# Hybrid pooling and short-convolution block, 256 tokens by 4096 channels: the parked gate product, the corner sums and the turned quarter share one 8 KB tile, and small work is moved in time

## The chip, the core and the metric
The kernel runs on one core of one Trainium2 chip. Time is device time in microseconds (us). The kernel before takes 2443.77 us, the median of three runs (2441.69 to 2444.59).

Engines: TensorE (PE; PEld is its load of the stationary operand), VectorE (DVE), ScalarE (ACT), GpSimd (POOL) and SyncE (SP). SP and POOL here mostly issue DMAs, each in the order of its own queue. Each engine executes its instructions in program order, so an instruction that waits holds up all behind it on that engine.

## The reference, cut to what matters
```python
def reference(x, norm_w, w_in, pool_w, pool_scale, conv_w, conv_b, gate_b, w_branch, w_out, final_norm_w):
    b, s, d = x.shape                                   # 1, 256, 4096
    for l in range(DEPTH):                              # 1
        h = rmsnorm(x, norm_w[l])
        proj = jnp.einsum('bsd,de->bse', h, w_in[l])    # 4096 -> 20480
        u_p, z_p, u_c, b_c, c_c, z_c, g_logit = jnp.split(proj, SPLIT_POINTS, axis=-1)
        y_pool = causal_multiscale_pool(u_p, pool_w[l], pool_scale[l]) * jax.nn.silu(z_p)
        y_conv = causal_gated_shortconv(u_c, b_c, c_c, conv_w[l], conv_b[l]) * jax.nn.silu(z_c)
        ys = jnp.stack([y_pool, y_conv], axis=2)
        br = jnp.einsum('bsnc,ncd->bsnd', ys, w_branch[l])          # 2 x (2048 -> 4096)
        gates = jax.nn.sigmoid(g_logit.reshape(b, s, N_BRANCHES, d) + gate_b[l])
        merged = jnp.sum(gates * br, axis=2)
        x = x + jnp.einsum('bsd,de->bse', merged, w_out[l])
    return rmsnorm(x, final_norm_w)
```
All is float32. The two branches (`n` = 0 pooling, 1 convolution) are each multiplied by a gate and added: `merged = g0*p0 + g1*p1`, 4096 channels wide.

## The kernel before, in words
**Units and steps.** Every matrix product is cut into units of 1024 output columns, and a unit into steps of 256 input channels. The units, in order: the convolution branch's `cz0 cb0 cu0 cc0 cz1 cb1 cu1 cc1`, the pooling branch's `pz0 pu0 pz1 pu1`, the gates `g0_0 g1_0 g0_1 ... g1_3` (branch, column quarter), the branch products `b0_0 b1_0 b0_1 ... b1_3`, and the output `o0` to `o3`. Units of w_in and w_out have 16 steps, branch units 8. A plain step (P) has 24 matmuls of 128x512, each float32 product being three products of rounded high and low halves; a step of Strassen's kind (S) has 21, seven products in place of eight. A text such as `SIX4` or `B0` gives a unit's steps; the gates' usual unit has 360 matmuls, `g1_3`, `cz1`, `pz0` and `o0` have 366, a `b0` unit ("PPPPPSPS") 186 and a `b1` unit ("PSPSPSPP") 183.

**Weights.** SP loads each step's 1 MB of weights into `raw`, three slots used in rotation. For a step, ACT rounds the weights to the high halves (`highs`, L54, `ring<-raw`) and DVE subtracts to get the low halves (`lows`, L57, `ring<-raw,ring`) into `ring`, 15 cells, of which a P step takes 4 and an S step 3 + 4. For S steps DVE first makes four sums in `parts`. A slot of `raw` is free for the next load when the step's lows are made; a cell of `ring` when the matmuls have read it. Preparation runs at most some three steps ahead of PE.

**The ends of units.** Banks `sums` (E) and `shared` (F) collect the results. At a unit's end ACT copies the E banks to `E` (or `Y`): `E<-sums`. The F banks ("corners") are copied to a slot, summed there by DVE (`corner_sums`) and added to `E` (`combine`). That slot (`join`) is one of the three of `raw`, in its turn in the rotation, unless `rotates` is off: the `b0` units use the tile `last_pair` (8 KB a partition).

**Work beside the product.** A unit's epilogue is a list of items; one is issued every tick (TICK, six matmuls). `silu`, transposes, the three taps of the convolution (`taps(j)`, four pairs of channel blocks, in `cz1` for `cc0` and in `pz0` for `cc1`), the bias gathers and sigmoids of the gates are such items. Gates are stored to `gates_d` in DRAM and come back later. In a `b0` unit's epilogue the product E*Y (branch times gate) is parked in `last_pair`; in a `b1` unit's it is E*Y, plus the parked product, then transposed on PE and stored to `m_d`. Both gates are loaded into Y (`before`), after the seventh of eight steps of the unit they belong to.

**Operands.** The stationary operands lie in `arena` (one more in `last_pair`, region LAST): first x, replaced by y (both branches' results, from `y_d`) during `g1_3` and `b0_0`, and by the merged rows (from `m_d`) from `b0_3` to `o0`. A `Fill` fetches 256 KB by POOL into `sa` or `sb`; at the earliest LANDING ticks later it is worked off one phase a tick: for a plain operand ACT rounds, then DVE subtracts; for one of S kind DVE makes four sums, ACT rounds, DVE subtracts.

**Opening.** In `cz0` x comes in 16 pieces in the order FIRST; pieces 0 to 7 are plain (`x_direct`), 8 to 15 staged (`x_scale` on ACT, `x_sums` on DVE, before the step that uses them). The rows of x, four of 1 MB, are fetched into E for the sum of squares (`fetch_rows`, `square`).

Of the kernel before, what the change touches and what calls it, by code (L numbers as in the profile page):

```python
# [10 lines left out]
F32R = mybir.dt.float32r  # L11
BF16 = mybir.dt.bfloat16
AF = mybir.ActivationFunctionType
# [6 lines left out]
NU = 1024  # L20
# [11 lines left out]
TAIL = 3  # L32

SIX5 = "PPPPPSPSPSPSPSPS"
FIRST = (0, 8, 9, 1, 10, 11, 2, 12, 13, 3, 14, 15, 4, 5, 6, 7)
OPENED = 10
SIX4 = "PPPPSPSPSPSPSPSP"
SEVEN3 = "PPPSPSPSPSPSPSPS"
EIGHT = "PSPSPSPSPSPSPSPS"
# [7 lines left out]
def hybrid_block(ctx: ExitStack, tc: tile.TileContext, x, xc, prm, rows_in, w_in, pool_w, w_branch, w_out, out):  # L47
# [5 lines left out]
    def act(dst, src, func=AF.Copy, **kw):  # L53
        return pin(nc.scalar.activation(dst, src, func, **kw))  # L54
# [4 lines left out]
    def mul(dst, a, b):  # L59
        return tt(dst, a, b, ALU.mult)  # L60

    def add(dst, a, b):
        return tt(dst, a, b, ALU.add)

    def sub(dst, a, b):
        return tt(dst, a, b, ALU.subtract)
# [7 lines left out]
    def move(dst, src):  # L74
        return pin(nc.gpsimd.dma_start(dst, src))
# [15 lines left out]
    E = sb("E", [P, 2, NU])  # L91
    Y = sb("Y", [P, 2, NU])
# [11 lines left out]
    gates_d = dram.tile([2, 4, P, 2, NU], F32, name="gates_d")  # L104
    g_d = dram.tile([2, P, 2, NU], F32, name="g_d")
    y_d = dram.tile([2, 2, P, 4, 2, T], F32, name="y_d")
    m_d = dram.tile([4, P, 4, 2, T], F32, name="m_d")
    o_d = dram.tile([3, P, 2, NU], F32, name="o_d")

    xrows = xf.rearrange("(t p) d -> p t d", p=P)  # L110
# [254 lines left out]
    def shared(i):  # L365
        return PF[i]
# [48 lines left out]
    def transposes(src, done):  # L415
        items = []
        for j in range(4):
            def f(j=j):
                for i in range(2):
                    for t in range(2):  # L420
                        c = (2 * j + i) * P
                        pin(nc.tensor.transpose(shared(j)[:, i * T + t * P:i * T + (t + 1) * P],  # L422
                                                src[:, t, c:c + P], ident))
                done(j)
            items.append(f)
        return items

    def pairs(items):
        return [lambda a=a, b=b: (a(), b()) for a, b in zip(items[::2], items[1::2])]

    def put(dst, src):
        for k in range(2):
            move(dst[:, :, 1 - k], src.rearrange("p (q k) t -> p q k t", k=2)[:, :, k])

    def chan(tile_):
# [12 lines left out]
    def make_ops(kinds):  # L448
# [33 lines left out]
    def conv_units(c, first):  # L482
        base = 2 * HALF + c * NU

        def b_epi(u):
            def copy(j):
                act(chan(Y)[:, 2 * j:2 * j + 2], bankview(j))
            return gap(6) + transposes(E, copy) + [lambda: move(g_d[c], Y)]

        def c_epi(u):  # L490
            def copy(j):
                if j == 3:
                    for i in range(4):
                        act(chan(E)[:, 2 * i:2 * i + 2], bankview(i))

            def taps(j):
                v, y = chan(E)[:, 2 * j:2 * j + 2], chan(Y)
                for i in range(2):
                    b = 2 * j + i
                    kb = 8 * c + b  # L500
                    act(y[:, b], v[:, i], AF.Identity, scale=tap_col(2, kb), bias=bias_col(kb))
                for i in range(2):
                    b = 2 * j + i
                    kb = 8 * c + b
                    for s in (1, 2):
                        stt(y[:, b, s:], v[:, i, 0:T - s], tap_col(2 - s, kb), y[:, b, s:], ALU.mult, ALU.add)

            items = gap(6) + pairs(transposes(E, copy)) + gap(2)
            for j in range(4):
                items += [lambda j=j: taps(j), None]  # L510
            return items + [lambda: move(E, g_d[c])] + gap(6) + [lambda: mul(Y, Y, E), lambda: put(y_d[1, c], chan(Y))]

        in_unit(f"cz{c}", base + 3 * HALF, lambda u: silu_y(), FIRST if first else SIX4, dst=Y)
        in_unit(f"cb{c}", base + HALF, b_epi, EIGHT).urgent = lambda: mul(E, E, Y)
        in_unit(f"cu{c}", base, lambda u: gap(2) + band_items(0) if c == 0 else [], SEVEN3, dst=Y)
        in_unit(f"cc{c}", base + 2 * HALF, c_epi, EIGHT).urgent = lambda: mul(E, E, Y)
# [100 lines left out]
    def gate_unit(n, c):  # L617
        def epi(u):
            def bias(t):
                gather(E[:, t], gate_b[n, None, c * NU:(c + 1) * NU].to_broadcast([P, NU]))  # L620

            return gap(1) + [lambda: bias(0), lambda: bias(1)] + gap(12) + [
                lambda: act(E[:, 0], E[:, 0], AF.Sigmoid), None,
                lambda: act(E[:, 1], E[:, 1], AF.Sigmoid), lambda: move(gates_d[n, c], E)]
        text = HOST if (n, c) == (0, 0) else SIX4 if (n, c) == (1, 3) else EIGHT
        in_unit(f"g{n}_{c}", 6 * HALF + n * D + c * NU, epi, text)

    def branch_unit(n, c):
        def epi(u):
            if n == 0:  # L630
                return gap(1) + [lambda: mul(parked_sum(), E, Y)]

            def copy(j):
                act(chan(Y)[:, 2 * j:2 * j + 2], bankview(j))

            def stored():
                put(m_d[c], chan(Y))
                merged[c] = now[0] + STORED
            return [lambda: mul(E, E, Y), None, add_parked] + gap(11) + pairs(transposes(E, copy)) + [stored]

        def add_parked():
            add(E, E, parked_sum())
            if c == 3:
                last_pair["stack"].close()
                open_last(F32R)
                last_pair["dtype"] = F32R

        text = B1 if n else B0
        u = Unit(f"b{n}_{c}", lambda i: w_branch[n, c, i], seq_y(text), y_ops[n], epi,
                 before=lambda: move(Y, gates_d[n, c]))  # L650
        u.urgent, u.lead = (lambda: None), 3
        if n == 0:
            u.rotates = False
        units.append(u)

    def parked_sum():
        return last_pair["tile"].rearrange("p (a n) -> p a n", a=2)

    merged = {}

# [25 lines left out]
    def copy(dst, src):  # L686
        return pin(nc.vector.tensor_copy(dst, src))
# [7 lines left out]
    class Fill:  # L695
# [9 lines left out]
        def advance(self):  # L705
            o, q = self.o, self.st[:, 0:self.o.n] if self.o.kind == "S" else self.st[:, 4:8]
            if self.phase == 0 and o.kind == "S":
                sums_s(self.st)
                self.phase = 1
            elif self.phase < 2:  # L710
                act(o.view[:, 0], q)
                self.phase = 2
            else:
                sub(o.view[:, 1], q, o.view[:, 0].bitcast(F32))
                self.phase = 3
                o.ready = True
                fills.remove(self)
# [1 line left out]
    stages = [sa]  # L719
    fills = deque()  # L720
    now = [0]
    LANDING, STORED = 6, 7

    def pop_fill(force=None):
        now[0] += 1
# [43 lines left out]

    def freed(o):  # L770
        if o.region == LAST:
            return lambda: "dtype" in last_pair
        return lambda: all(p.left == 0 for p in o.prev)

    warm = op.tile([P, 2 * P], BF16, name="warm")
# [17 lines left out]
        stt(r, m, 1.5, r, ALU.add, ALU.mult)  # L793

    def fetch_rows(c):
        move(E, xrows[:, :, c * NU:(c + 1) * NU])

    def square(c):
        q = E
# [2 lines left out]

    first_order = FIRST
    xt = Y.rearrange("p a n -> p (a n)").rearrange("p (s o c) -> p s o c", s=4, c=P)
# [194 lines left out]
    for u in units:  # L999
# [129 lines left out]
```

## Time and profile before
| | |
|---|---|
| median of 3 runs | 2443.77 us |
| the profiled execution's own time | 2441.96 us |
| its span, first to last instruction | 2440.2 us |
| mean granted clock of TensorE | 0.993 |
| PE busy, 10515 matmuls | 2382.4 us, 98% |
| DVE busy | 2130.3 us, 87% |
| ACT busy | 1430.8 us, 59% |
| POOL busy | 86.3 us, 4% |
| DMA moved | 547.07 MB, 224 GB/s mean |

The sum of the prediction is made against the profiled execution (2441.96 us, of which 1.8 us lie around the span). In the views, "a<-b" is what an instruction writes and reads, by the program's names; the helpers ACT L54 and DVE L57 record nearly everything those engines do, so groups are told apart by tiles. Idle time stands in brackets with what ended it. The view of stretches of time gives, for each engine, busy time and number of instructions in that stretch, then the granted clock, the DMA engines' busy share and GB/s.

### The profile page before, as it was taken

The page shows a single profiled execution, that of the slowest core. Times are in us where ns is not written, and L with a number is a line of the kernel's source. Part 1 is how long each engine was busy: PE and PEld are TensorE (multiplying, and loading weights), DVE is VectorE, ACT ScalarE, POOL GpSimd, SP SyncE. Part 2 cuts the span into 40 slices and gives each one's busy share as a digit, 9 for nine tenths or more (in the row PEclk, how much of TensorE's full clock was granted, in tenths as well). Part 3 has the DMA queues.
Part 4 walks back from the last instruction along what each step waited for, and adds up shares of the span by engine and source line. Part 5 has one row for each costly group of instructions (what it writes and reads, how often), then busy time and mean ns, then how long its engine had stood idle before and what let it go on. Part 6 is the DMA issues. An engine that isn't in the chain of part 4 may idle for free. (4 is left out here: it accounts for less than half of the span.)

```text
span 2440.2 us, 26870 instructions
## 1 busy us (share of the span) xinstructions
PE 2382.4 (98%) x10515; PEld 1959.1 (80%) x10515; DVE 2130.3 (87%) x1756; ACT 1430.8 (59%) x1380; POOL 86.3 (4%) x148
## 2 busy tenths in 40 slices
PE   8999999999999999999999999999899999899998
PEld 6888887888878888888888888887678887778886
DVE  8789989988989879879999999888788789799998
ACT  5655656656556556556666566655555556456664
POOL 0000000000000000000000000000000001000000
PEclk9999999999999999999999999999999999999999
DMA  8656556555646555555676567667656656658667
GB/s 320 232 190 228 194 187 245 215 205 192 226 182 229 207 206 191 207 208 193 238 258 236 197 239 256 225 211 256 221 214 251 250 204 235 216 197 281 236 222 265
DMA packets 82959, 547.07 MB, mean 224 GB/s; under 512 B 9488, under 2 KB 9488, under 8 KB 21776
## 3 DMA queue, kind: packets, MB, share of 16 engines
q1 hardware_dynamic: 69120, 484.47, 54.2%
q0 software_dynamic: 13280, 59.78, 7.9%
q8 instruction: 82, 1.34, 0.2%
q10 hardware_dynamic: 432, 1.11, 0.1%
q14 instruction: 45, 0.37, 0.0%
HBM read 519.10 MB, written 26.21 MB: 223 GB/s over the span
## 5 line engine op out<-in xcount | busy, mean ns | idle before, releaser
L935 PE MATMUL sums<-ring,arena 128*128 128x512 f32 x7515 | 1760.0, 391 | 38.2 <-ACT E L54 17.9
L935 PEld LDWEIGHTS sums<-ring,arena 128*128 128x128 f32 x7515 | 1411.4, 188 | 340.7 <-DVE ring L57 21.9
L57 DVE TENSOR_TENSOR ring<-raw,ring 128x2048 fp32r<-128x2048 f32 (+3 forms) x526 | 938.8, 1796 | 186.4 <-ACT ring L54 182.7
L54 ACT ACTIVATE ring<-raw 128x2048 fp32r<-128x2048 f32 (+3 forms) x526 | 790.7, 1519 | 491.5 <-PE sums L935 259.5
L54 ACT ACTIVATE ring<-parts 128x1024 fp32r<-128x1024 f32 (+1 forms) x403 | 399.9, 1007 | 355.4 <-DVE parts L57 322.8
L935 PE MATMUL shared<-ring,arena 128*128 128x512 f32 x2100 | 509.5, 391 | 5.0 <-DVE ring L57 5.0
L57 DVE TENSOR_TENSOR ring<-parts,ring 128x2048 fp32r<-128x2048 f32 (+3 forms) x225 | 434.9, 1945 | 50.3 <-ACT ring L54 49.4
L935 PEld LDWEIGHTS shared<-ring,arena 128*128 128x128 f32 x2100 | 395.4, 189 | 91.0 <-DVE ring L57 8.7
L57 DVE TENSOR_TENSOR parts<-parts,raw 128x512 f32<-128x512 f32 x378 | 262.0, 693 | 12.9
L57 DVE TENSOR_TENSOR parts<-raw 128x1024 f32<-128x1024 f32 x189 | 230.6, 1220 | 8.0 <-DMA raw<-in_w_in_dram 7.1
L935 PE MATMUL sums<-ring,last_pair 128*128 128x512 f32 x366 | 89.8, 396 | 0.0
L935 PEld LDWEIGHTS sums<-ring,last_pair 128*128 128x128 f32 x366 | 68.9, 188 | 16.5
L57 DVE TENSOR_TENSOR raw<-raw 128x512 f32<-128x512 f32 (+1 forms) x78 | 67.7, 868 | 11.1 <-ACT raw L54 9.3
L54 ACT ACTIVATE raw<-shared 128x512 f32<-128x512 f32 x104 | 55.8, 606 | 2.8 <-DVE ring L57 2.1
L54 ACT ACTIVATE E<-sums,rin 128x512 f32<-128x512 f32 x56 | 36.4, 686 | 25.5 <-PE sums L935 25.4
L935 PE MATMUL shared<-ring,last_pair 128*128 128x512 f32 x168 | 41.6, 396 | 0.0
L935 PEld LDWEIGHTS shared<-ring,last_pair 128*128 128x128 f32 x168 | 31.6, 188 | 7.7
L69 DVE SCALAR_TENSOR_TENSOR E<-raw,rin,E 128x1024 f32<-128x1024 f32 x28 | 34.7, 1280 | 0.2
L54 ACT ACTIVATE arena<-sa 128x512 fp32r<-128x512 f32 (+2 forms) x16 | 12.2, 760 | 32.9 <-DMA sa<-y_d 15.1
L78 POOL DMA_DIRECT2D E<-in_rows_dram x16 | 13.9, 867 | 432.9 <-DVE E L69 430.8
L54 ACT ACTIVATE arena<-sb 128x512 fp32r<-128x512 f32 (+1 forms) x15 | 11.3, 754 | 25.8 <-DVE sb L57 20.9
L57 DVE TENSOR_TENSOR E<-E,Y 128x2048 f32<-128x2048 f32 x11 | 25.2, 2290 | 0.3
(116 smaller groups left out, 566.8 us busy)
## 6 DMA issues: line engine op xcount, KB each, us to landing
raw<-in_w_in_dram SPq DMA_DIRECT2D x319, 1024.0 KB, 4.8
raw<-in_w_branch_dram SPq DMA_DIRECT2D x64, 1024.0 KB, 4.9
raw<-in_w_out_dram SPq DMA_DIRECT2D x64, 1024.0 KB, 5.0
E<-in_rows_dram POOLq DMA_DIRECT2D x16, 512.0 KB, 11.3
gates_d<-E POOLq DMA_DIRECT2D x8, 1024.0 KB, 8.3
Y<-gates_d POOLq DMA_DIRECT2D x8, 1024.0 KB, 6.2
Y<-in_xc_dram SPq DMA_DIRECT2D x16, 256.0 KB, 5.9
E<-in_x_dram POOLq DMA_DIRECT2D x4, 1024.0 KB, 6.5
```

The lines of the kernel that those rows point to most:

```text
L54: return pin(nc.scalar.activation(dst, src, func, **kw))
L57: return pin(nc.vector.tensor_tensor(out=dst, in0=a, in1=b, op=op))
L69: return pin(nc.vector.scalar_tensor_tensor(out=dst, in0=a, scalar=s, in1=b, op0=op0, op1=op1, **kw))
L78: return pin(nc.gpsimd.dma_start(dst, src, accum_op=ALU.add))
L935: pin(nc.tensor.matmul(ps, lhs, rhs, start=n == 0, stop=n == u.total[b] - 1))
```

## The change
Seven edits, in the order of the words in the diff:

1. FIRST takes the pieces of x in another order: the second step's piece is now a plain one, and staged pieces stand at places 2, 4, 6, 7, 9, 10, 12, 14 (counted from 0) in place of 1, 2, 4, 5, 7, 8, 10, 11. OPENED goes from 10 to 12 with it.
2. The four `taps` stand at ticks 11, 17, 25 and 33 of the epilogue in place of 11, 13, 15 and 17.
3. `p0`, the first branch times its gate, stays in Y (`Y = E*Y`). `last_pair` takes in turn: the corners of both branches, the second gate, and the turned quarter (for c < 3; the last one is turned in Y). So `b1` units too have `rotates` off, and no slot of `raw` serves as corner slot from `b1_0` to `b1_3`.
4. The gates' loads move: the first gate of quarter 0 is loaded right after the last gate is stored, those of quarters 1 to 3 at the twelfth tick of the `b0` unit before use; the second gate is loaded into `last_pair` at the first tick after the `b1` unit. Its product (`gated`) is at tick 8 and the sum with Y at tick 9, where both were in ticks 1 and 3. The transposes stay where they were.
5. A fill of S kind is rounded by DVE (`copy`, a cast) in the same tick as its subtraction; ACT no longer takes part.
6. LANDING goes from 6 to 8 ticks.
7. The first row fetch of x goes through SP (`load`), where it stands behind the loads of the first seven weight tiles; the other three stay on POOL.

```diff
-FIRST = (0, 8, 9, 1, 10, 11, 2, 12, 13, 3, 14, 15, 4, 5, 6, 7)
-OPENED = 10
+FIRST = (0, 1, 8, 2, 9, 3, 10, 11, 4, 12, 13, 5, 14, 6, 15, 7)
+OPENED = 12
...
-            items = gap(6) + pairs(transposes(E, copy)) + gap(2)
-            for j in range(4):
-                items += [lambda j=j: taps(j), None]
+            items = gap(6) + pairs(transposes(E, copy)) + gap(1)
+            for j, n in enumerate((1, 5, 7, 7)):
+                items += gap(n) + [lambda j=j: taps(j)]
...
-                lambda: act(E[:, 1], E[:, 1], AF.Sigmoid), lambda: move(gates_d[n, c], E)]
+                lambda: act(E[:, 1], E[:, 1], AF.Sigmoid), lambda: move(gates_d[n, c], E)] + (
+                    [lambda: move(Y, gates_d[0, 0])] if (n, c) == (1, 3) else [])
...
     def branch_unit(n, c):
         def epi(u):
             if n == 0:
-                return gap(1) + [lambda: mul(parked_sum(), E, Y)]
+                return gap(1) + [lambda: mul(Y, E, Y)]
+            turned = spare() if c < 3 else Y
+
+            def gated():
+                mul(E, E, spare())
+                if c == 3:
+                    last_pair["stack"].close()
+                    open_last(F32R)
+                    last_pair["again"] = True
...
-            return [lambda: mul(E, E, Y), None, add_parked] + gap(11) + pairs(transposes(E, copy)) + [stored]
+            return [lambda: move(spare(), gates_d[1, c])] + gap(6) + [gated, lambda: add(E, E, Y), None,
+                lambda: c < 3 and move(Y, gates_d[0, c + 1])] + gap(3) + pairs(transposes(E, copy)) + [stored]
...
-        u = Unit(f"b{n}_{c}", lambda i: w_branch[n, c, i], seq_y(text), y_ops[n], epi,
-                 before=lambda: move(Y, gates_d[n, c]))
-        u.urgent, u.lead = (lambda: None), 3
-        if n == 0:
-            u.rotates = False
+        u = Unit(f"b{n}_{c}", lambda i: w_branch[n, c, i], seq_y(text), y_ops[n], epi)
+        u.urgent, u.lead, u.rotates = (lambda: None), 3, False
...
-            elif self.phase < 2:
+            elif self.phase == 0:
                 act(o.view[:, 0], q)
                 self.phase = 2
             else:
+                if self.phase == 1:
+                    copy(o.view[:, 0], q)
                 sub(o.view[:, 1], q, o.view[:, 0].bitcast(F32))
...
-    LANDING, STORED = 6, 7
+    LANDING, STORED = 8, 7
...
     def fetch_rows(c):
-        move(E, xrows[:, :, c * NU:(c + 1) * NU])
+        (move if c else load)(E, xrows[:, :, c * NU:(c + 1) * NU])
```

More of the change, by code (lines that the diff above doesn't have):

```diff
@@ L623, in epi, with spare @@
                 lambda: act(E[:, 0], E[:, 0], AF.Sigmoid), None,
-                lambda: act(E[:, 1], E[:, 1], AF.Sigmoid), lambda: move(gates_d[n, c], E)]
+                lambda: act(E[:, 1], E[:, 1], AF.Sigmoid), lambda: move(gates_d[n, c], E)] + (
+                    [lambda: move(Y, gates_d[0, 0])] if (n, c) == (1, 3) else [])
         text = HOST if (n, c) == (0, 0) else SIX4 if (n, c) == (1, 3) else EIGHT
         in_unit(f"g{n}_{c}", 6 * HALF + n * D + c * NU, epi, text)
+    def spare():
+        return last_pair["tile"].rearrange("p (a n) -> p a n", a=2)
     def branch_unit(n, c):
@@ L630, in epi @@
             if n == 0:
-                return gap(1) + [lambda: mul(parked_sum(), E, Y)]
+                return gap(1) + [lambda: mul(Y, E, Y)]
[6 more added lines that the diff above has]
+                    last_pair["again"] = True
             def copy(j):
-                act(chan(Y)[:, 2 * j:2 * j + 2], bankview(j))
+                act(chan(turned)[:, 2 * j:2 * j + 2], bankview(j))
             def stored():
-                put(m_d[c], chan(Y))
+                put(m_d[c], chan(turned))
                 merged[c] = now[0] + STORED
-            return [lambda: mul(E, E, Y), None, add_parked] + gap(11) + pairs(transposes(E, copy)) + [stored]
[L641 to L646, printed above, removed]
-        text = B1 if n else B0
-        u = Unit(f"b{n}_{c}", lambda i: w_branch[n, c, i], seq_y(text), y_ops[n], epi,
-                 before=lambda: move(Y, gates_d[n, c]))
-        u.urgent, u.lead = (lambda: None), 3
-        if n == 0:
-            u.rotates = False
+            return [lambda: move(spare(), gates_d[1, c])] + gap(6) + [gated, lambda: add(E, E, Y), None,
+                lambda: c < 3 and move(Y, gates_d[0, c + 1])] + gap(3) + pairs(transposes(E, copy)) + [stored]
+        text = B1 if n else B0
+        u = Unit(f"b{n}_{c}", lambda i: w_branch[n, c, i], seq_y(text), y_ops[n], epi)
+        u.urgent, u.lead, u.rotates = (lambda: None), 3, False
         units.append(u)
-    def parked_sum():
-        return last_pair["tile"].rearrange("p (a n) -> p a n", a=2)
     merged = {}
@@ L771, in freed @@
         if o.region == LAST:
-            return lambda: "dtype" in last_pair
+            return lambda: "again" in last_pair
         return lambda: all(p.left == 0 for p in o.prev)
```

## The prediction
> **What bounds the kernel now.** I read the page's first part, then who PE waited for, then the chain of waits for PE's own pace, then busy time by stretches cut at the ends of units.
>
> ```profile
> PE 2382.4 (98%) x10515; PEld 1959.1 (80%) x10515; DVE 2130.3 (87%) x1756; ACT 1430.8 (59%) x1380; POOL 86.3 (4%) x148
> ```
> ```profile
> PE sums L935 <- ACT E L54: 17.9, 3, 8.7
> ```
> ```profile
> 2355.80 7.48 PE sums L935 x33
> ```
> ```profile
> 8.00:12.00 4.00, 2.28 (x10) 1.57 (x9) 1.14 (x3) 1.40 (x3) 0.00 (x0) 1.00 1.04 412
> 24.00:28.00 4.00, 4.00 (x19) 3.28 (x18) 3.93 (x9) 1.68 (x1) 0.00 (x0) 1.00 0.74 267
> ...
> 350.00:438.70 88.70, 85.93 (x384) 70.00 (x383) 81.16 (x74) 52.71 (x56) 2.05 (x3) 1.00 0.59 214
> 686.90:775.70 88.80, 85.80 (x383) 70.14 (x382) 80.89 (x71) 52.59 (x55) 2.01 (x3) 1.00 0.59 214
> ...
> 1629.30:1726.80 97.50, 85.18 (x368) 68.11 (x367) 80.92 (x79) 55.42 (x55) 8.77 (x15) 0.97 0.68 237
> 1726.80:1772.90 46.10, 44.85 (x186) 36.30 (x186) 33.10 (x29) 23.09 (x23) 4.44 (x7) 0.95 0.75 253
> 1772.90:1819.60 46.70, 43.86 (x184) 35.50 (x185) 41.15 (x29) 28.19 (x29) 0.53 (x1) 0.96 0.54 195
> ...
> 1863.50:1906.10 42.60, 42.02 (x185) 34.22 (x184) 38.76 (x26) 25.09 (x23) 0.54 (x1) 1.00 0.55 197
> ...
> 2036.60:2093.50 56.90, 44.10 (x184) 34.89 (x182) 44.97 (x44) 30.17 (x31) 3.21 (x6) 0.94 0.51 186
> 2093.50:2182.50 89.00, 87.53 (x382) 71.34 (x383) 78.02 (x74) 49.47 (x48) 4.19 (x7) 0.98 0.61 219
> ```
>
> PE bounds the kernel: 7.48/33 = 0.227 us a matmul, and nothing in the change takes a matmul away. What can be won is what units lose on that pace. `g1_3` (row 1629.30): 366 x 0.227 = 83.0 of 97.5, 14.5 lost. `b0_0` (1726.80): 42.2 of 46.1, 3.9 lost, 2.3 of them a granted clock of 0.95. `b1_0` (1772.90): 41.5 of 46.7, while `b1_1` (1863.50), the same 183 matmuls, takes 42.6. `b1_3` (2036.60): 41.5 of 56.9, 15.4 lost. `cz1` and `pz0` (350.00, 686.90): 2.8 and 3.0 idle. PE's longest wait, 8.7, was for ACT's copies of the banks to E.
>
> **The change, part by part.** Terms are us against the profiled 2441.96, which is 1.8 below the median of the runs.
>
> *A, opening: row fetch and order of x.* The fetch is 1 MB on POOL at 1.52; PE's second step waits on lows that wait on weights.
>
> ```profile
> 1.52 0.84 POOL L75 DMA_DIRECT2D E<-in_x_dram  x1 [0.15 <-issue]
> ```
> ```profile
> 14.24 1.91 ACT L54 ACTIVATE ring<-raw 128x2048 fp32r<-128x2048 f32 x1 [1.60 <-DMA raw<-in_w_in_dram]
> ```
>
> The DMA engines are full there (share 1.04 at 412 GB/s in 8-12), so without the fetch the weights land 1.05/412 = 2.5 us earlier. On SP it comes after seven weight tiles, at some 25 us, where the share is 0.74; the next weights come up to 2.5 late there, with two prepared steps (10.9 us) as cover. The new order of pieces puts a cheap piece first; DVE did not hold PE there, so I cost it at nothing. The Trainium skill, "Trainium Kernel Development and Optimization", Key Constraints, says that DMAs of the SP, ACT and POOL queues share the same 16 engines and that the issuing queue saves only issue time; by that alone A is 0 and the sum ends 2.5 higher. The trace agrees on the shared engines (1.04), but shows room later (0.74). A = 2.5, ends 0 and 4.5 (with a shorter dip of the clock).
>
> *C, the end of g1_3.* ACT's order, then DVE's:
>
> ```profile
> 1711.96 0.95 ACT L54 ACTIVATE arena<-sb 128x896 fp32r<-128x896 f32 x1 [4.74 <-DVE sb L57]
> ...
> 1723.41 0.95 ACT L54 ACTIVATE arena<-sa 128x896 fp32r<-128x896 f32 x1 [4.96 <-issue]
> 1724.27 1.89 ACT L54 ACTIVATE ring<-raw 128x2048 fp32r<-128x2048 f32 x1
> 1726.07 1.25 ACT L54 ACTIVATE E<-sums,rin 128x512 f32<-128x512 f32 x2
> ```
> ```profile
> 1705.83 0.69 DVE L57 TENSOR_TENSOR arena<-sa,arena 128x512 fp32r<-128x512 f32 x1
> ...
> 1708.71 2.29 DVE L57 TENSOR_TENSOR ring<-raw,ring 128x2048 fp32r<-128x2048 f32 x1
> 1710.91 1.01 DVE L57 TENSOR_TENSOR sb<-sb 128x128 f32<-128x128 f32 x4
> 1712.94 1.09 DVE L57 TENSOR_TENSOR arena<-sb,arena 128x896 fp32r<-128x896 f32 x1 [1.02 <-ACT arena L54]
> 1714.74 2.29 DVE L57 TENSOR_TENSOR ring<-raw,ring 128x2048 fp32r<-128x2048 f32 x1 [0.71 <-ACT ring L54]
> ```
> ```profile
> raw<-in_w_branch_dram SPq DMA_DIRECT2D x64, 1024.0 KB, 4.9
> ```
> ```profile
> L687 DVE CAST arena<-sa 128x896 fp32r<-128x896 f32 (+1 forms) x7 | 4.5, 636 | 0.2
> L54 ACT ACTIVATE arena<-sa 128x512 fp32r<-128x512 f32 (+2 forms) x16 | 12.2, 760 | 32.9 <-DMA sa<-y_d 15.1 <-DVE sa L57 11.3 <-issue 5.0
> ```
>
> ACT waits twice for a fill's sums on DVE, and the copies PE waits for stand behind. Both ACT roundings go. What is late next: the `ring<-raw` before the copies, whose slot of `raw` is free when the lows of 1714.74 are made. In the new order DVE does lows (2.3 from 1708.7, 0.7 earlier as the plain subtraction of 1705.83 moves behind), sums, cast and subtraction (1.0 + 0.6 + 1.1), these lows: done near 1715.4 in place of 1717.0. Load 4.9, rounding 1.9, first copy 0.6: PE starts at 1722.8, not 1726.8. C = 4.0. Ends: 2.4 (only ACT's block) and 8.4 (no wait). A wait of 4.7 stays, so I leave the clock's dip of 2.3 in `b0_0`.
>
> *D, b0_0 and b1_0.* LANDING 8 gives a fill two ticks more to land (six matmuls a tick, 2.7 us) and so spares ACT most of its waits for them (15.1 in the row above). The last of the sixteen fills ends in the program's order 40 ticks before it is used, so slower fills cost nothing; with that cover gone each tick would be 1.4. ACT's wait of 1.3 at the end of `b0_0` (46.10 - 44.85) and the 4.1 of `b1_0` over `b1_1` come of the same lag and of two 1 MB gate transfers that stay. Half goes: D = 2.8, ends 0 and 5.4. Of `b1_0`'s 4.1, 1.9 is a clock of 0.96 after waits of 2.8. The Trainium skill, "TensorE: Matmul & The Clock Gate", Part 1, has the clock fall after an idle window of some 3.4 us; by it this dip should not be, and the 1.9 would be no dip to win back (sum 0.9 higher). The row has it, and I go by the row.
>
> *E, b1_3 and the start of o0.*
>
> ```profile
> 2037.47 0.95 ACT L54 ACTIVATE arena<-sa 128x896 fp32r<-128x896 f32 x1 [2.09 <-DVE sa L57]
> ...
> 2085.39 2.00 ACT L54 ACTIVATE ring<-raw 128x1536 fp32r<-128x1536 f32 x2 [7.99 <-DMA raw<-in_w_out_dram]
> 2090.23 0.95 ACT L54 ACTIVATE arena<-sa 128x896 fp32r<-128x896 f32 x1 [2.84 <-DVE sa L57]
> ...
> 2092.88 2.04 ACT L54 ACTIVATE E<-sums 128x512 f32<-128x512 f32 x4
> ```
> ```profile
> 2074.85 0.54 POOL L75 DMA_DIRECT2D Y<-gates_d  x1
> ```
> ```profile
> 2073.95 2.29 DVE L57 TENSOR_TENSOR ring<-raw,ring 128x2048 fp32r<-128x2048 f32 x1
> ```
>
> The corner slot sat in `raw`, so only two tiles were under way, and the load ACT needs was issued after the lows of 2073.95 (2076.3, landing 9.1 later at 2085.39, beside the 1 MB gate load of 2074.85). Now it goes a step earlier, that gate load has left, and the next tile takes this place: 2076.3 + 4.9 + 1.9 = 2083.1, when the banks close (of the 17.9 waited for ACT E, 8.7 is at C and 1.3 at D, so 7.9 here: last matmul 2093.5 - 7.9 = 2085.6, the first bank nine matmuls, 2.0, before). The fill's 2.84 is gone. Wait 7.9 to 0.3, plus 1.1 of clock (89.0 x 0.02 = 1.8, some left): 8.7. Inside `b1_3` ACT is free 2.09 + 0.95 earlier, DVE has sums and a cast (1.65) more on the way: 1.2. E = 9.9, ends 4 and 13.
>
> *F, casts.* Thirteen of 0.64 go to DVE, 8.3 us, and leave ACT. Where DVE has room they cost nothing; `g1_3` (80.9 of 83.0) and `o0` (78.0 of some 85) have none to spare for 2.6 and 4. I take -1.0; ends 0 and -6.
>
> *J, the second gate.* POOL issues its load when `combine` is done; nothing POOL must do soon stands behind it (the next gate, later stores). DVE waits for it in order, behind it an S step's preparation and the sum that PE's transposes need:
>
> ```profile
> 1907.55 2.29 DVE L57 TENSOR_TENSOR E<-E,raw 128x2048 f32<-128x2048 f32 x1
> ...
> 1922.96 1.22 DVE L57 TENSOR_TENSOR parts<-raw 128x1024 f32<-128x1024 f32 x1
> 1924.22 1.42 DVE L57 TENSOR_TENSOR parts<-parts,raw 128x512 f32<-128x512 f32 x2
> 1925.56 1.75 DVE L57 TENSOR_TENSOR ring<-raw,ring 128x1536 fp32r<-128x1536 f32 x1
> ```
> ```profile
> 1926.47 1.03 PE L422 MATMUL shared<-ident,E 128*128 128x128 f32 x8
> ```
> ```profile
> DMA to landing us min/median/max: 5.0/7.9/10.2
> ```
>
> From the unit's start (1906.07): `combine` ends at 3.8, then landing, 2.3 product, 2.6 + 1.75 preparation, 2.3 sum: 12.8 plus landing, 17.8 to 23.0, and transposes at 20.4. The last row is over the sixteen transfers of gates. At the median 20.7, 0.3 late; at the slowest 2.6. J = -1.5 over four places; ends 0 and -10.
>
> *B, taps spread.* Same instructions, later. At 350-439 DVE is busy 81.2, against PE's 83.0 plus transposes:
>
> ```profile
> 377.34 3.75 DVE L69 SCALAR_TENSOR_TENSOR Y<-E,par,Y 128x255 f32<-128x255 f32 x8
> ```
>
> Two taps are 3.75, four 7.5, the product after them 2.3. A pair of P and S steps gives PE 45 x 0.227 = 10.2 and costs DVE 2.29 + 2.64 + 1.75 + 2.29 = 9.0 (four cells as at 1708.71, the rest as in the rows of J), so DVE gains 1.2 a pair. Moving three taps back by 8 to 22 us and the product by 20 lets it gain some 1 us more before the work is due: B = 1.0 a unit, 2.0 together. Ends: 0, and 2.3 a unit.
>
> Sum: 2.5 + 2.0 + 4.0 + 2.8 + 9.9 - 1.0 - 1.5 = 18.7; 2441.96 - 18.7 = 2423.3, beside the median 2425.1.
>
> **The rivals.**
> - *All waits fall.* A 4.5, B 4.6, C 8.4 with its dip 2.3, D 5.4, E 9.9, J and F -2.5: 32.6, 2411. For it: with two engines coupled less, one late load should not recur. Against: DVE's 81 of 83.
> - *The corner slot was not it.* If the weights for `o0` land as late (9 and not 4.9), E shrinks by 7: 2432. For it: what slowed that load to 9.1 is inferred. Against: 4.9 is the median of 64, and the gate load beside it is gone.
> - *VectorE takes it all.* B 0, C 2.4, D 0, A 2.5, E 6, casts -6, J -3: 1.9, 2442, no change that a measurement of this kernel tells (0.2% is 4.9 us).
> - *Slower: the gate's load holds DVE.* At four places, each us of landing above 7.6 is one on PE's transposes. To end 4.9 above before it must eat 18.7 + 1.5 + 4.9 = 25, 6.3 each: landings of 13.9. The slowest shown is 10.2, with 10.4 in all; beyond it, 2450 and more.
>
> **How the numbers follow.** Forecast 0.47 (its own range 2417 to 2432), all waits fall 0.20, the slot not it 0.15, VectorE 0.10, slower 0.08. Predicted is 2425. The range, 2409 to 2441, reaches to the second and the fourth case; below it 0.06, above it 0.13. Faster 0.82, same 0.10, slower 0.08.
>
> **What would show it.** A: the second step's first matmul near 13.7 and not 16.2 (14.24 plus 1.91). C: no ACT wait for DVE `sa` or `sb`, PE's wait at the start of `b0_0` near 4.7. E: `o0` starts without a wait on ACT E. J: PE transposes waiting for DVE E, under 1 us each. Idle in `cz1` and `pz0` near 1.8 each. Wrong if the transposes wait 3 us or more, if `o0` still waits 4 for ACT E, or if `g1_3` and `o0` grow by the casts.

## The result, and the profile after

| | before | changed |
|---|---|---|
| median | 2442.73 us, 4 runs (2441.18 to 2444.59) | 2419.74 us, 4 runs (2418.02 to 2420.86) |
| ratio, 95% interval | | 0.9905 (0.9888 to 0.9922) |
| the profiled execution, its span | 2441.96, 2440.2 us | 2420.03, 2418.3 us |

The changed kernel is 23.0 us faster. Predicted were 2425, with 2409 to 2441 as the range. The page's first part and PE's waits (in total, how often, the longest) of the changed kernel:

```profile
PE 2379.8 (98%) x10515; PEld 1960.6 (81%) x10515; DVE 2137.6 (88%) x1769; ACT 1421.8 (59%) x1367; POOL 85.6 (4%) x147
```
```profile
PE sums L937 <- DVE ring L57: 9.4, 5, 3.7
PE sums L937 <- ACT E L54: 7.5, 2, 7.1
...
PE shared L422 <- DVE E L57: 2.1, 3, 1.2
```

PE's waits for ACT's copies to E were 17.9 in three places and are 7.5; one long one of 7.1 is left. The casts show as 13 more instructions on DVE and 13 fewer on ACT. The same stretches as in the prediction, cut at the first matmuls of `cz1`, `pz0`, `g1_3`, `b0_0`, `b1_0`, `b0_3`, `b1_3` and `o0` and rounded to 0.1:

```profile
349.80:436.00 86.20, 85.78 (x384) 69.99 (x382) 80.06 (x72) 51.27 (x56) 2.05 (x3) 1.00 0.61 220
684.30:770.80 86.50, 85.88 (x384) 70.04 (x383) 79.97 (x69) 51.10 (x54) 2.02 (x3) 1.00 0.61 219
1624.50:1715.60 91.10, 83.65 (x368) 68.48 (x366) 82.04 (x78) 51.96 (x51) 8.78 (x15) 0.98 0.74 254
1715.60:1760.00 44.40, 44.07 (x187) 36.05 (x187) 35.45 (x35) 22.35 (x22) 4.47 (x7) 0.96 0.75 262
1760.00:1806.60 46.60, 43.78 (x184) 35.40 (x185) 41.82 (x29) 28.65 (x29) 0.00 (x0) 0.96 0.60 210
1979.60:2024.50 44.90, 44.22 (x203) 36.51 (x203) 35.90 (x28) 26.21 (x31) 5.29 (x9) 1.00 0.75 275
2024.50:2072.70 48.20, 44.55 (x184) 36.31 (x183) 46.02 (x46) 27.49 (x28) 2.69 (x5) 0.93 0.56 201
2072.70:2160.70 88.00, 85.58 (x384) 70.28 (x383) 82.20 (x80) 44.75 (x42) 4.72 (x8) 1.00 0.62 220
```

Beside the prediction's rows this is where the 21.9 us of span went: `cz1` -2.5, `pz0` -2.3, `g1_3` -6.4, `b0_0` -1.7, `b1_0` -0.1, `b1_3` -8.7, `o0` -1.0, and `b0_3` +0.9 (44.0 before). The opening hardly moved in this execution. What still holds PE at the end of `g1_3` stands in ACT's order (timeline of the changed kernel: start, duration, instruction, idle before it and what ended that):

```profile
1705.05 1.08 ACT L54 ACTIVATE raw<-shared 128x512 f32<-128x512 f32 x2
1713.05 1.91 ACT L54 ACTIVATE ring<-raw 128x2048 fp32r<-128x2048 f32 x1 [6.91 <-DMA raw<-in_w_branch_dram]
1714.86 2.41 ACT L54 ACTIVATE E<-sums,rin 128x512 f32<-128x512 f32 x4
```

No fill is left there. ACT waits 6.91 for the weights of `b0_0`'s third step, and the copies that PE needs stand behind that rounding. The slot of `raw` for these weights came free when DVE had made these low halves, at 1706.3 (1704.02 + 2.29):

```profile
1704.02 2.29 DVE L57 TENSOR_TENSOR ring<-raw,ring 128x2048 fp32r<-128x2048 f32 x1
```

### The profile page after: what moved, and what is told of

The parts are those of the page before. It is cut to its first block, busy times and chain, and to the rows that moved or that the text cites. A ratio compares the mean times of both kernels' runs of the same rounds, so it can differ in the third digit from the quotient of the medians.

```text
span 2418.3 us, 26848 instructions
## 1 busy us (share of the span) xinstructions
PE 2379.8 (98%) x10515; PEld 1960.6 (81%) x10515; DVE 2137.6 (88%) x1769; ACT 1421.8 (59%) x1367; POOL 85.6 (4%) x147
## 5 line engine op out<-in xcount | busy, mean ns | idle before, releaser
L57 DVE TENSOR_TENSOR raw<-raw 128x512 f32<-128x512 f32 (+1 forms) x66 | 57.3, 868 | 10.9 <-ACT raw L54 9.3
L54 ACT ACTIVATE raw<-shared 128x512 f32<-128x512 f32 x88 | 47.0, 606 | 0.3
L54 ACT ACTIVATE last_pair<-shared 128x512 f32<-128x512 f32 x44 | 24.2, 600 | 13.8 <-PE shared L422 13.1
L57 DVE TENSOR_TENSOR E<-E,last_pair 128x2048 f32<-128x2048 f32 x12 | 27.4, 2287 | 2.2 <-ACT E L54 2.2
L54 ACT ACTIVATE E<-sums 128x512 f32<-128x512 f32 x44 | 25.6, 596 | 2.9 <-PE sums L937 0.5
```

Of the source, the lines that this page charges most:

```text
L57: return pin(nc.vector.tensor_tensor(out=dst, in0=a, in1=b, op=op))
```

## The experiments

Each kernel below is the changed kernel with the edit shown. The unit times are from first matmul to first matmul of the profiled execution, in us.

| | before | changed | taps bunched | corners in raw | casts on ACT | landing 6 | both fill edits undone |
|---|---|---|---|---|---|---|---|
| time, median | 2442.7 | 2419.7 | 2422.4 | 2445.5 | 2423.1 | 2415.7 | 2429.3 |
| `cz1` | 88.8 | 86.1 | 88.8 | 86.4 | 87.0 | 86.9 | 87.3 |
| `pz0` | 88.8 | 86.4 | 88.7 | 86.6 | 86.4 | 87.0 | 86.1 |
| `g1_3` | 97.4 | 91.1 | 90.2 | 93.9 | 92.2 | 94.8 | 97.7 |
| `b0_0` | 46.2 | 44.4 | 45.2 | 44.0 | 45.8 | 44.7 | 46.4 |
| `b1_0` | 46.6 | 46.6 | 45.2 | 45.1 | 45.2 | 42.5 | 46.7 |
| `b0_1`, `b0_2`, each | 44.0 | 44.0 | 44.0 | 49.7, 49.3 | 44.0 | 44.0 | 44.0 |
| `b0_3` | 44.0 | 44.9 | 44.9 | 50.3 | 44.9 | 44.9 | 44.9 |
| `b1_3` | 56.9 | 48.2 | 47.9 | 54.4 | 49.3 | 46.0 | 50.1 |
| `o0` | 89.0 | 87.9 | 88.4 | 92.9 | 87.8 | 86.4 | 87.9 |

How far can one column be trusted? In the kernels of this section whose edits don't concern the unit, `cz1` takes 86.1 to 87.3, `pz0` 86.1 to 87.1, `g1_3` 90.2 to 93.9, `b0_0` 44.0 to 45.2, `b1_0` 45.1 to 46.7, `b1_3` 47.4 to 48.2 and `o0` 87.9 to 89.0. Each ratio below has an interval of some 0.0015 to either side, 3.6 us, so a difference of 4 us between two changed kernels isn't secured by the times alone.

**The taps in their old place.**
```diff
-            items = gap(6) + pairs(transposes(E, copy)) + gap(1)
-            for j, n in enumerate((1, 5, 7, 7)):
-                items += gap(n) + [lambda j=j: taps(j)]
+            items = gap(6) + pairs(transposes(E, copy)) + gap(2)
+            for j in range(4):
+                items += [lambda j=j: taps(j), None]
```


> The changed kernel with the four taps back at ticks 11, 13, 15 and 17; all else as changed. In the profile of the changed kernel cz1 and pz0 are 2.6 and 2.4 us shorter than before, where 1.0 each was forecast. Theory: the spread of the taps did all of that, since VectorE falls less far behind; then cz1 takes 88.8 and pz0 88.8 again, PE waits there for the low halves again, and the time is some 4.9 above the changed kernel's 2419.7: 2424.6. Rival (the forecast's step, 1.0 a unit, the rest from elsewhere): 2421.7 with units of 87.2.

Measured: 2422.44 (0.9922 of before, 0.9905 to 0.9938). The two units of this kernel:

```profile
346.70:435.50 88.80, 86.01 (x383) 70.06 (x382) 81.12 (x74) 52.79 (x57) 2.05 (x3) 1.00 0.59 215
683.80:772.50 88.70, 85.78 (x383) 70.11 (x382) 80.94 (x71) 52.58 (x55) 2.01 (x3) 1.00 0.61 214
```

Both are back where they were: 2.6 and 2.3 us in this pair of executions are the taps' place alone, 1.5 to 2.7 over the spread of the units above. The whole time rose by 2.7 and not by 4.9, and the unit `cz1` starts at 346.7 here, at 349.8 in the changed kernel, although the opening is the same code. The stretch from 6 to 45.5 us, of this kernel and of the changed one, shows it:

```profile
6.00:45.50 39.50, 37.68 (x151) 30.23 (x152) 34.07 (x54) 26.79 (x35) 0.84 (x1) 1.00 0.92 356
```
```profile
6.00:45.50 39.50, 35.74 (x138) 28.57 (x139) 33.51 (x53) 25.24 (x33) 0.84 (x1) 0.91 0.92 351
```

With the clock at 1.00 PE has done 13 matmuls more by the same time (13 x 0.227 = 3.0 us). That granted clock differs from one execution to the next, so single spans here carry some 3 us that no edit made; units, with their spread above, are the better measure.

**The corners of the b1 units back in raw.**
```diff
-        u.urgent, u.lead, u.rotates = (lambda: None), 3, False
+        u.urgent, u.lead, u.rotates = (lambda: None), 3, n == 1
```


> The changed kernel with the corners of the b1 units back in a slot of raw; the tile keeps the second gate and the turned quarter. Theory: the slot missing from the rotation delayed the weights that stand ahead of ACT's last copies; then PE waits for ACT E at the start of o0 again, 4 to 8 us, o0's start moves back by as much and the time is 2424 to 2428. Rival: the first gate's 1 MB load beside those weights was the cause, and it is gone in this kernel too; then o0 starts without a wait and the time is 2420 to 2421.

Measured: 2445.47 (1.0011, 1.0002 to 1.0020): the whole gain of the change is gone, and more. PE's waits and two stretches, `b0_1` and `b1_3`:

```profile
PE shared L422 <- DVE E L57: 15.0, 5, 4.7
PE sums L937 <- ACT E L54: 13.5, 2, 7.2
```
```profile
1804.20:1854.00 49.80, 45.84 (x204) 37.96 (x203) 34.33 (x23) 24.13 (x26) 3.12 (x5) 0.97 0.66 244
2038.60:2093.00 54.40, 44.38 (x185) 35.85 (x183) 48.07 (x48) 26.30 (x27) 3.21 (x6) 0.92 0.49 177
```

The wait at the start of `o0` is back (13.5 - 7.2 = 6.3), by an edit of the slot alone. But the rival cause isn't absent here. The gate load beside the late weights in the kernel before was that of the second gate, which edit 4 moves and doesn't remove, and in this kernel it stands beside them again:

```profile
2078.21 0.53 POOL L75 DMA_DIRECT2D last_pair<-gates_d  x1
```
```profile
2080.84 0.33 SPq L72 DMA_DIRECT2D raw<-in_w_out_dram  x1
```
```profile
2090.53 1.91 ACT L54 ACTIVATE ring<-raw 128x2048 fp32r<-128x2048 f32 x1 [6.21 <-DMA raw<-in_w_out_dram]
```

The copies that PE waits for stand behind this rounding. Its weights took some 9.6 to land (2080.84 to 2090.4), where the median of these loads in the changed kernel is 4.8. So the free slot is what takes the wait away, but how much of the 6.3 is the later issue and how much the gate's load beside it, this run doesn't separate. Neither theory had the other 19 us. They come at four places, `b0_1` to `b0_3` and `o0`, from 5.0 to 5.8 each, and ACT's and DVE's orders in `b0_1` show how:

```profile
1812.77 1.92 ACT L54 ACTIVATE ring<-raw 128x2048 fp32r<-128x2048 f32 x1 [7.42 <-DMA raw<-in_w_branch_dram]
```
```profile
1814.72 4.56 DVE L57 TENSOR_TENSOR ring<-raw,ring 128x2048 fp32r<-128x2048 f32 x3 [6.80 <-ACT ring L54]
1819.20 2.28 DVE L57 TENSOR_TENSOR E<-E,last_pair 128x2048 f32<-128x2048 f32 x1
...
1825.65 2.28 DVE L57 TENSOR_TENSOR E<-E,Y 128x2048 f32<-128x2048 f32 x1
```

Weights that come late hold ACT, then DVE's low halves for 6.80, and behind these in DVE's order stand the product with the second gate and the sum that PE's transposes need. In the kernel before, with the corners in `raw` too but the product at tick 1, ACT waited as long for the same weights, and `b0_1` took 44.0:

```profile
1827.90 1.92 ACT L54 ACTIVATE ring<-raw 128x2048 fp32r<-128x2048 f32 x1 [7.51 <-DMA raw<-in_w_branch_dram]
```

So the product at tick 8 (edit 4) makes the kernel sensitive to late weights, and the free slot (edit 3) keeps them early: the first is only good with the second. (No run has the free slot without the late product.)

**The fills' rounding back on ACT, the landing back at 6 ticks, and both.**
```diff
-            elif self.phase == 0:
+            elif self.phase < 2:
                 act(o.view[:, 0], q)
                 self.phase = 2
             else:
-                if self.phase == 1:
-                    copy(o.view[:, 0], q)
...
-    LANDING, STORED = 8, 7
+    LANDING, STORED = 6, 7
```


> The changed kernel with the rounding of S-kind fills back on ACT, a phase of its own again; the fill's landing stays at 8 ticks. Theory: at the end of g1_3 the roundings that wait for VectorE's sums held ACT's copies; then PE's wait at the start of b0_0 grows from 7.1 to about 9 and VectorE's waits inside g1_3 (4.7 before, 0.5 changed) return in part: g1_3 95 to 97 instead of 91.1, the time 2423 to 2426. Rival: it was the later landing that took them away; then g1_3 stays within 1 of 91.1 and the time within 1.5 of 2420, less up to 1 for VectorE's relief in o0.

> The changed kernel with the fills' landing back at 6 ticks. Theory: the two ticks spare ACT its waits for fills' transfers; then ACT's idle time for sa and sb grows by some 10 us over the fills, b0_0 goes from 44.4 back to some 46, and the time is 2421.5 to 2423. Rival: ACT had room for these waits once the casts had left it; then every unit stays within 0.5 and the time within 1 of 2420.

> The changed kernel with both edits of the fills undone: rounding of S-kind fills on ACT and landing at 6 ticks. Undone alone, the first made g1_3 1.1 longer and the second 3.75, of the 6.4 that the whole change took from it. Theory: the two overlap, and either one alone removes most of ACT's waits for fills; then with both undone g1_3 takes 96.5 to 97.5 as before, and the time is 2422 to 2425. Rival: they add, and the other 1.5 in g1_3 came from elsewhere in the change (the gate loads that have left its end); then g1_3 takes 95.5 to 96.3, b1_0 and b1_3 are short as with the landing alone, and the time is about 2419.

Measured: 2423.09 (0.9922, 0.9907 to 0.9937), 2415.67 (0.9889, 0.9875 to 0.9904) and 2429.27 (0.9946, 0.9929 to 0.9963). As a square:

| | landing 6 | landing 8 |
|---|---|---|
| rounding on ACT | 2429.3 | 2423.1 |
| rounding on DVE | 2415.7 | 2419.7 |

The two edits overlap so far that the longer landing, beside the moved rounding, is a loss. With the rounding on ACT it gains 6.2; with the rounding on DVE it loses 4.1. The rounding's move gains 13.6 by itself and 3.4 beside the longer landing. The 4.1 isn't secured by the ratios (0.9889 and 0.9905); what supports it is `b1_0`, 42.5 against 45.1 to 46.7, where PE's wait at the fourth step is 0.6 in place of 2.8. The expectation for the landing alone was wrong on both sides; that for the rounding had the time and not `g1_3` (95 to 97); that for both had `g1_3` within 0.2 and not the time, which is 4 above its range. `g1_3` of the three, in this order, and then `b1_0` with the landing at 6:

```profile
1625.30:1717.50 92.20, 83.99 (x368) 68.39 (x366) 80.23 (x75) 54.10 (x53) 8.78 (x15) 0.97 0.73 251
```
```profile
1624.60:1719.40 94.80, 84.55 (x368) 68.15 (x366) 84.76 (x84) 52.70 (x51) 9.30 (x16) 0.97 0.72 245
...
1764.10:1806.60 42.50, 41.92 (x184) 34.19 (x183) 39.90 (x27) 26.13 (x25) 0.00 (x0) 1.00 0.60 213
```
```profile
1623.30:1720.90 97.60, 86.42 (x367) 69.31 (x365) 80.82 (x79) 55.31 (x54) 8.78 (x15) 0.96 0.68 237
```

With both undone `g1_3` takes its old time, so these two edits made all of its gain. The longer landing moves fills out of `g1_3` (DVE busy 84.76 there with 6 ticks, 82.04 with 8) and into `b0_0`: the last fill is subtracted 32.6 us after that unit's start in the changed kernel, 22.5 us with the shorter landing. There it pushes back the preparation of `b1_0`, which pays 4.1: 2.2 of wait, and most of the rest is the fall of the clock behind that wait, which came in this execution and not in others with the same wait (45.2 with the taps bunched). `b1_3` and `o0` take 2.2 and 1.5 more; that they pay in the same way, for the merged rows, is inferred from the sizes and not shown.

**The opening: the row fetch on POOL, and then also the old order of x.**
```diff
-        (move if c else load)(E, xrows[:, :, c * NU:(c + 1) * NU])
+        move(E, xrows[:, :, c * NU:(c + 1) * NU])
```
The second kernel has this and the former FIRST and OPENED.

> The changed kernel with the first row fetch of x back on POOL, where it is issued early, beside the first weights. Theory: the fetch takes its megabyte of the full DMA engines; the second step's matmuls then start some 2 us later than with it on SP, as the forecast has it (2.5), and the time is 2421.5 to 2422.5. Rival: as the profile of the changed kernel read, 1.2 earlier in landing and none of it left at the end of cz0: the time stays within 1 of 2419.7.

> The changed kernel with the whole opening as before: the first row fetch on POOL and the pieces of x in the former order. Theory: the order of the pieces is worth nothing, so this is the row fetch alone again, 2421.5 to 2422.5 if that counts and 2419 to 2421 if not. Rival: the former order, with a staged piece second, is the better cover for x; then the time is 2418 or less, and cz0 is shorter by more than 1.

Measured: 2421.55 (0.9921, 0.9904 to 0.9937) and 2421.72 (0.9919, 0.9904 to 0.9934). PE's first matmul of the second step in the changed kernel, with the fetch on POOL, and with the whole old opening:

```profile
15.04 0.50 PE L937 MATMUL sums<-ring,arena 128*128 128x512 f32 x1 [1.94 <-ACT ring L54]
```
```profile
16.73 0.49 PE L937 MATMUL sums<-ring,arena 128*128 128x512 f32 x1 [0.16 <-ACT ring L54]
```
```profile
16.90 0.51 PE L937 MATMUL sums<-ring,arena 128*128 128x512 f32 x1 [0.95 <-ACT ring L54]
```

The fetch is worth 1.7 at that matmul and about 1.8 in the medians (2421.55 - 2419.74). The ratios differ by 0.0016 with intervals of that width, so by the times alone the gain is likely and not secured. The kept traces secure its place: in the eleven kernels with the fetch on SP this matmul comes at 13.84 to 15.04 (14.5 in the mean), in the three with it on POOL, the kernel before among them, at 16.21 to 16.90 (16.6). Of these 2.1, 1.6 are left in the mean at the start of `cz1`. The order of x adds 0.2 to the medians, which is nothing.

**The product of a b0 unit later.**
```diff
-                return gap(1) + [lambda: mul(Y, E, Y)]
+                return gap(18) + [lambda: mul(Y, E, Y)]
```
DVE's order at the start of `b1_0` in the changed kernel was the reason for this one:

```profile
1765.51 2.67 DVE L57 TENSOR_TENSOR last_pair<-last_pair 128x512 f32<-128x512 f32 x3
1768.10 2.28 DVE L57 TENSOR_TENSOR ring<-raw,ring 128x2048 fp32r<-128x2048 f32 x1
1770.30 2.28 DVE L57 TENSOR_TENSOR E<-E,last_pair 128x2048 f32<-128x2048 f32 x1
1772.62 2.29 DVE L57 TENSOR_TENSOR Y<-E,Y 128x2048 f32<-128x2048 f32 x1
...
1779.08 2.29 DVE L57 TENSOR_TENSOR ring<-parts,ring 128x2048 fp32r<-128x2048 f32 x1
```

There is no idle time between them, and `Y<-E,Y` isn't needed before the next unit.

> The changed kernel with the product of a b0 unit's result and its gate moved from the second to the nineteenth tick of the epilogue. In the profile of the changed kernel it stands on VectorE (2.3 us) between the corner sums and the preparation of the b1 unit's fourth step, which PE waits for: 2.8 in b1_0, 0.6 in b1_1 and b1_2, 3.7 in b1_3, with a fall of the clock behind the two long ones. Theory: each wait shrinks by up to 2.3 (6.2 in all at most) and the falls of the clock in b1_0 and b1_3 go with them (1.7 to 3.4 each): 2409 to 2414. Rival: VectorE has the work to do anyway and PE waits as long for a later step, or for the sum that the transposes need: within 2 of 2419.7.

Measured: 2413.66 (0.9886, 0.9871 to 0.9901), 6.1 below the changed kernel. `b1_0` and `b1_3`:

```profile
1760.40:1803.10 42.70, 42.24 (x185) 34.10 (x185) 40.88 (x28) 28.31 (x29) 0.00 (x0) 1.00 0.60 215
2018.90:2064.40 45.50, 42.73 (x185) 33.86 (x183) 44.40 (x41) 26.23 (x27) 2.69 (x5) 1.00 0.59 204
```

They were 46.60 and 48.20, and the falls of the clock (0.96 and 0.93) went with the waits. `b1_1` and `b1_2` are 1.1 shorter each. In `o0` 1.7 came back: the transposes wait 2.7 there.

**The third step of b0_0 after the end of g1_3.**
```diff
-    last_x = units[-1]
+    last_x = units[-1]; last_x.urgent = lambda: None
```
With `urgent` set, preparation runs two steps ahead (`lead`) during the unit's last step, and not more.

> The changed kernel with one thing added: the third step of b0_0 is prepared only after the end of g1_3, so that ACT's copies of the banks no longer stand behind a rounding that waits for weights. PE's wait there is 7.1 in the profile of the changed kernel. Theory: the wait falls to 1 or less and the fall of the clock behind it goes: 2412 to 2415. Rival: the wait moves to the third step of b0_0, whose low halves now stand behind combine on VectorE (weights landed at 1713, lows some 6 later, the step due 11 after the unit's start): 2417 to 2420.

Measured: 2415.03 (0.9888, 0.9873 to 0.9903), 4.7 below. ACT's copies and the stretches of `g1_3` and `b0_0`:

```profile
1707.37 2.79 ACT L54 ACTIVATE E<-sums,rin 128x512 f32<-128x512 f32 x4 [0.22 <-PE sums L937]
1712.66 1.92 ACT L54 ACTIVATE ring<-raw 128x2048 fp32r<-128x2048 f32 x1 [2.50 <-DMA raw<-in_w_branch_dram]
```
```profile
1624.10:1709.30 85.20, 83.70 (x368) 68.46 (x367) 78.06 (x74) 51.14 (x50) 8.81 (x15) 1.00 0.72 245
1709.30:1755.20 45.90, 43.14 (x187) 34.46 (x185) 39.24 (x39) 23.41 (x22) 4.48 (x7) 1.00 0.88 302
```

The copies now stand in front of that rounding and wait for nothing but PE, and `g1_3` is 5.9 shorter. `b0_0` gives 1.5 back, at its sixth step and not at its third: some of the rival, in another place.

**The three together**, with the product at the twenty-third tick and the transposes two ticks later (three in `o0`); then with the landing at 6; then with the taps at ticks 11, 16, 23 and 30.

> Three edits on the changed kernel: the third step of b0_0 prepared after the end of g1_3 (4.7 below the changed kernel when done alone), the product of a b0 unit with its gate at the twenty-third tick in place of the second (6.1 below when done alone at the nineteenth), and the transposes of the merged quarters two ticks later, three in o0 (PE waited there 0.7 in b0_3 and 1.2 to 2.7 in o0). Theory: the three act at different places and add: 2419.7 - 4.7 - 6.1 - 2 = 2407, range 2404 to 2410. Rival: what VectorE is relieved of in one place it owes in the next, so that the gains overlap: 2411 to 2414, with PE's waits for the low halves in b1_3 and o0 longer than the 1.5 and 1.2 of the late product alone.

> The three edits and the fills' landing at 6 ticks. Alone on the changed kernel the shorter landing gave 4.0: 4.1 in b1_0, 2.2 in b1_3 and 1.5 in o0, against 3.75 lost in g1_3. Theory: the late product has taken what there was to win in b1_0 (2.8 of waits), so the loss in g1_3 decides and this is 0 to 3 slower than the three edits alone. Rival: earlier fills relieve VectorE at places of their own, and it is 2 to 4 faster.

> The three edits and the taps at ticks 11, 16, 23 and 30 in place of 11, 17, 25 and 33. PE waits 0.5 to 1.5 at the start of cb1 and of pu0 for ACT's copies to Y, since Y's last use is later with the taps spread. Theory: three ticks (4.1 us) earlier frees Y in time and the two waits go: 1 to 2 faster than the three edits alone, cz1 and pz0 within 0.5. Rival: VectorE falls behind again within the units, by as much: within 1 of the three edits alone.

Measured: 2404.53 (0.9851, 0.9835 to 0.9867), 2405.59 (0.9851, 0.9835 to 0.9868) and 2403.71 (0.9844, 0.9829 to 0.9858). They do not cancel one another: 15.2 below the changed kernel, 37.6 below the one before, where the first two alone gave 4.7 and 6.1. The transposes' move and the product's four further ticks weren't run alone, so the other 4.4 isn't divided. PE's waits of the first:

```profile
PE sums L937 <- DVE ring L57: 5.6, 5, 1.8
...
PE sums L937 <- ACT E L54: 1.9, 2, 1.1
```

Landing 6 costs 3.1 in `g1_3` (87.7 against 84.6) and 1.3 in `b1_3`, gains 2.5 in `b0_0`, and is no longer distinguishable in the whole. With the earlier taps no wait for ACT Y over 0.4 is left at `cb1` and `pu0` (0.6 and 0.7 without), but 0.8 us can't be told from nothing.

## Why the prediction was right or wrong

The direction, the range and the main mechanism held; the sum was 18.7 and the spans differ by 21.9. That the sum came so close is in part luck: C measured 2.4 and B 2.8 more than forecast, D and E 1.0 and 0.2 less, and A nothing in this execution. By its steps, each with the size in the profiled execution:

- *A, opening (2.5).* In the profiled execution nothing was left of it at `cz1`: the second step's matmul came at 15.04 and not near 13.7, 1.2 earlier than before, and a longer fall of the clock took this back. Over all kept traces the mechanism holds, with 2.1 at that matmul and 1.6 at `cz1`; the term was somewhat too large, and smaller than what the clock adds or takes in one execution. That the order of x costs nothing was right.
- *B, taps (2.0).* It measured 4.8 (3.2 to 5.3 over the spread). The mechanism was right (the bunched taps restore the units), the size wrong: "VectorE gains some 1 us more before the work is due" should have been nearly the whole wait, 2.3 a unit, the end that was named and not taken.
- *C, end of g1_3 (4.0).* It measured 6.4 (3.5 to 7.2 over the spread). The late next was named rightly: the `ring<-raw` before the copies. But its load took 6.7 (slot free at 1706.3, landed at 1713.05) and not the median 4.9, so the wait fell only from 8.7 to 7.1, not to 4.7. Most of the rest of the gain is matmuls held up for low halves inside the unit, 4.7 before and 0.5 after, counted from start to start, which the sum left out though the fills' edits were bound to touch them.
- *D, b0_0 and b1_0 (2.8).* It measured 1.8, all but 0.1 of it in `b0_0`, where the fills' edits did it as forecast: with both undone the unit takes 46.4 again. `b1_0` gave nothing: its wait at the fourth step, 2.8, stands in both kernels. (Half of 1.3 + 4.1 is 2.7 and not 2.8.) The step that failed is "slower fills cost nothing", with the distance to the operand's use as cover. The operand was in time, but VectorE's work for it moved towards the preparation of `b1_0`. Beside the casts the landing of 8 loses 4.1.
- *E, b1_3 and o0 (9.9).* It measured 8.7 + 1.0. Without the free slot 6.2 of it in `b1_3` are lost again; without the fills' edits 1.9. The rival "the corner slot was not it" is out. The forecast had two causes for the 9.1 that the weights took to land, and the run with the slot undone has both of them again, the later issue and the gate's load beside it, so their shares stay open. `b1_3` still had a wait of 3.7 at its fourth step, which the product `Y<-E,Y` caused.
- *F, casts (-1.0).* No loss can be seen: `o0` takes 87.9 with the casts on VectorE and 87.8 without, `g1_3` 91.1 and 92.2. The term wasn't needed.
- *J, second gate (-1.5).* The waits for DVE E are 2.1, 0.2 of them in `cz1`, so 1.9; the place was right and the cause was not. The landing, 5.1 in the median for these four loads and not 7.9, was never the last: VectorE waited for no DMA on that tile. The sum stands behind an S step's preparation:

```profile
2087.84 1.22 DVE L57 TENSOR_TENSOR parts<-raw 128x1024 f32<-128x1024 f32 x1
...
2092.17 2.29 DVE L57 TENSOR_TENSOR E<-E,Y 128x2048 f32<-128x2048 f32 x1
```

- *The rival that ended slower* asked for 6.3 us at each of four places, by late gate loads. With the corners in `raw`, 5.0 to 5.8 at each of them did make the kernel slower, by late weights. The place was right and the price near it; the cause is another, and what prevents it is the free slot.

"VectorE takes it all" didn't come about. The prediction counted VectorE's room as an average; the runs show that the order of its instructions matters too, since moving 2.3 us of work by 17 ticks gave 6.1.

## What to carry to other kernels

Of an engine that works in order, look at what stands before the instruction that someone waits for, and move what isn't needed yet (here a product by 17 ticks, a rounding behind four copies): 6.1 and 4.7 us for edits of one line, where the engine's busy share said only that it is full. Test the edits of a change one by one against the whole, since they may need each other (the free slot and the late product) or replace each other, with the sign of the second perhaps turning (the casts and the landing). When timing a fill or a load, ask whose instruction is tied to its arrival, not only when its data are used.

## What was not expected of the hardware

The fall of the granted clock doesn't follow from the length of the wait. PE's wait of 3.65 at `b1_3`'s fourth step, in the changed kernel and in the one with the later third step:

```profile
2044.22 2.08 PE L937 MATMUL sums<-ring,arena 128*128 128x512 f32 x4 [3.65 <-DVE ring L57]
```
```profile
2039.42 1.43 PE L937 MATMUL sums<-ring,arena 128*128 128x512 f32 x5 [3.65 <-DVE ring L57]
```

The unit's clock is 0.93 in the first and 1.00 in the second. In the trace's records the clock falls to 0.50 for 3.41, 6.83 or 10.24 us, multiples of one length, and in each of the 14 traces all changes of the clock lie on one grid of 3.413 us, within 0.004. The Trainium skill, "TensorE: Matmul & The Clock Gate", Part 1, says that the window of 3413 ns runs freely and doesn't start with the kernel; the lengths agree, and the same wait ending differently is what a free-running window would give. The two waits, cut on that grid (the stretch, its length, then PE's busy time first):

```profile
2039.90:2043.31 3.41, 0.66 (x3) 0.20 (x2) 3.34 (x5) 1.78 (x2) 0.54 (x1) 1.00 0.33 94
2043.31:2050.14 6.83, 5.92 (x14) 4.68 (x15) 6.76 (x8) 4.03 (x4) 0.00 (x0) 0.50 0.52 163
```
```profile
2034.28:2037.69 3.41, 1.49 (x7) 0.91 (x5) 3.34 (x6) 1.06 (x1) 0.54 (x1) 1.00 0.45 108
2037.69:2041.11 3.42, 1.69 (x7) 1.42 (x8) 3.42 (x3) 3.32 (x4) 0.00 (x0) 1.00 0.30 67
```

In the first, one window holds most of the wait and PE is busy for 0.66 of it; the clock is at 0.50 in the next two. In the second the wait is split, 1.49 and 1.69 are busy, and no fall comes. The 14 traces, cut so from their first record of the full clock to 2390 us, bear this out: each of the 43 falls follows a window in which PE was idle for 1.82 us or more, and of some 9700 windows that no fall followed only two were as idle, the most 1.90. That a whole idle window is needed isn't borne out: in this kernel some 1.8 to 1.9 us idle within one window brought the fall, and a longer wait passed when the grid divided it.
